# A decoder block's residual turnings sixteen steps apart, later retention scores, and one write and four reads for both tiles of a turning

## Chip, cores, metric

The kernel runs on one core of one Trainium2 chip. The metric is the device time of that core in microseconds (us). Times of several runs are given as their median; the trace comes from one further, profiled execution.

## What is computed

A decoder block for 256 tokens (S), model width 2048 (D) and FFN width 5632, all in float32:

```python
h = h + 0.5 * swiglu(rms_norm(h, ffn1_norm), ffn1_w_gate, ffn1_w_up, ffn1_w_down)
n = rms_norm(h, mix_norm)
rq, rk, rv, rg, sq, sk, sv = split(n @ w_in)
ret = silu(rg) * groupnorm(retention(rope(rq), rope(rk), rv)) * ret_gn_gain   # 8 heads
swa = sliding_window_attention(rope(sq), rope(sk), sv, swa_sinks)             # 16 heads, window 128
h = h + concat(ret, swa) @ w_out
h = h + memory_cross_attention(rms_norm(h, xa_norm), rms_norm(mem, mem_norm), xa_wq, xa_wkv, xa_wo)
h = h + 0.5 * swiglu(rms_norm(h, ffn2_norm), ffn2_w_gate, ffn2_w_up, ffn2_w_down)
out = rms_norm(h, final_norm)
# swiglu(x, g, u, d) = (silu(x @ g) * (x @ u)) @ d
```

## The kernel before

**A stream of weight steps.** All the large products are one list of 772 steps. A step takes one 128 x 1024 piece of a weight matrix (512 KB) and does 12 matmuls of 128x512: two halves of the tokens (t = 0, 1), two pieces of 128 rows, and three matmuls for each fp32 product. `three` (L470 to L472) multiplies the high part of the activations with the high part of the weights (`wh`), the high part with the rest of the weights (`wl`), and the rest of the activations (`lo` in a `blk` tile) with `wh`. A `Unit` is the 4 to 12 steps that fill one PSUM tile `acc` (two of them alternate); when it ends, its `done` function is called.

**Preparing weights.** SP issues the loads: one DMA of 1 MB for two steps, `load_pair` (L203) or `load` (L197), into one of three `wf` tiles. `split` makes `wh` by a ScalarE copy (L71) and `wl` by a VectorE subtraction (L76), three steps ahead of the step that uses them (LOOKAHEAD), with four buffers each. Steps follow each other in program order on TensorE, ScalarE, VectorE and SP: the engines' orders are set when the program is built and no instruction overtakes another on its engine.

**Everything else** is put between the steps by `later(delay, fn)`: `fn` is called, and its instructions get their place, `delay` steps after the step at which `later` was called. SP issues the DMAs of such tasks in that same order, between its weight loads.

**Crossings.** Projections come out with tokens on the partitions, and the next product wants features there. `cross` (L434) turns a pair of 128x512 tiles: VectorE transposes each in squares of 32x32 into a 2 KB tile of the pool `t2k` (L444), a step later SP writes the two tiles to DRAM boxes (L449, 256 KB each), two steps after the start SP issues four reads for each box (L456, 64 KB each), which put the squares in place, and five steps after the start (TURN) the function `then` uses the result. It is used by `to_h` (residual additions), `up_done` (each block of gate-up products of an FFN), `rqk_done` (retention queries and keys), `put_done` (cross-attention queries and keys) and `turn_h`: 54 crossings in all. `turn_h` turns the residual `h` back to tokens on partitions for the last norm; `begin_ffn2` puts its four calls at 6, 10, 14 and 18 steps after the last product of the cross-attention (`xa_wo`), so at the start of the second FFN.

**Other pieces that the text names.** `Norm.finish` computes a row scale per token and `Norm.spread` (L412) lays it out over the partitions: two VectorE products (L417) and two TensorE transposes (L418). In retention `rqk_done` rotates queries and keys with VectorE (L730, L733); two and three steps later `ret_scores` (L740) does the score matmuls (L742, L743) and masks them on VectorE (L746, L747); `rv_done`'s `half` does the value matmuls (L761 to L764). `swa_group` (L606) does the sliding-window attention with VectorE and ScalarE; the product that divides the weights by their sum is L639, and five steps later TensorE transposes the weights (L646). In the tail `very_last` writes eight output tiles (L1000), all from `t2k`.

**Pools.** `t2k` has 10 tiles of 2 KB per partition, `blk` 13 of 8 KB, `wf` 3 of 8 KB, `wh` and `wl` 4 of 4 KB each; in PSUM there are two `acc` and four `tmp`.

Of the kernel before, what the change touches and what calls it, by code (L numbers as in the profile page):

```python
# [39 lines left out]
def decoder_block(ctx: ExitStack, tc: tile.TileContext, a: dict, out: bass.AP):  # L40
# [20 lines left out]
    def t2k(dt=F32):  # L61
        return work.tile([P, 512], dt, tag="t2k", name=nm("t2k"), bufs=10)

# [26 lines left out]
    nc.vector.tensor_copy(identr, ident)  # L90
    ones = const.tile([P, P], F32, tag="ones", name="ones")
    nc.vector.memset(ones, 1.0)
# [265 lines left out]
    class Norm:  # L358
# [39 lines left out]
        def finish(self):  # L398

            x = self.sums  # L400
            nc.vector.tensor_tensor(x[:, :S], x[:, :S], x[:, S:], ALU.add)
            tp = tmp_ps()
            for t in range(2):
                nc.tensor.matmul(tp[:, t : t + 1], x[:, t * P : (t + 1) * P], ones[:, :1], start=True, stop=True)
            ms = sm(2, "ms")
            nc.vector.tensor_scalar(ms, tp[:, :2], 1.0 / D, EPS, ALU.mult, ALU.add)
            nc.gpsimd.tensor_tensor(self.rs, ms, mhalf[:, :2], ALU.pow)
            self.ready = True
            if self.spreads:
                later(3, self.spread)  # L410

        def spread(self):  # L412

            tp = tmp_ps()
            for t in range(2):
                rep = t2k()[:, :P]
                nc.vector.tensor_scalar(rep, ones, self.rs[:, t : t + 1], None, ALU.mult)  # L417
                nc.tensor.transpose(tp[:, t * P : (t + 1) * P], rep, ident)  # L418
            self.rows = work.tile([P, S], F32, tag="rows", name=nm("rows"), bufs=1)
            copy(self.rows, tp[:, :S])  # L420

# [11 lines left out]

    def cross(src, then, room=None, delay=TURN):  # L434

        room = [None, None] if room is None else room
        boxes = []  # L440
        out = []
        sq = [t2k() for _ in src]
        for x, v in zip(sq, src):
            nc.vector.transpose(x.rearrange("p (g q j) -> p q g j", g=4, q=4), squares_of(v))  # L444

        def write():
            for x in sq:
                boxes.append(dram.tile([P, 512], F32, tag="box", name=nm("box")))
                nc.sync.dma_start(boxes[-1], x)  # L449

        def read():
            for box, dst in zip(boxes, room):
                dst = t2k() if dst is None else dst
                far = box.rearrange("(i r) (g n) -> g r i n", i=4, g=4)
                for g in range(4):
                    nc.sync.dma_start(dst[32 * g : 32 * g + 32, :].rearrange("p (i n) -> p i n", i=4), far[g])  # L456
                out.append(dst.rearrange("p (i q j) -> p q i j", i=4, q=4))
        later(1, write)
        later(2, read)
        later(delay, lambda: then(out))  # L460

# [13 lines left out]
    def to_h(w, lhs, factor, blocks, norm=None, then=None):  # L475

        def done(acc, b):
# [11 lines left out]
            else:  # L489
                s = [t2k() for _ in range(2)]  # L490
                for t in range(2):
                    copy(s[t], acc[:, t, :], scale=factor)
                cross(s, add, s)
        for b in range(4):
            Unit(w, b, 512, lhs, lambda acc, b=b: done(acc, b), blocks, pair=True)

    def ffn(norm, w_gate, w_up, down):
# [12 lines left out]
        def up_done(b):  # L510
            def done(acc):
# [4 lines left out]
                def made(out):  # L516
                    acts[b] = halves_of(out, blk())
                cross(s, made, s)
            return done
# [193 lines left out]
    def rqk_done(g, which):  # L713
        def done(acc):
            def finish(out):
# [18 lines left out]
                if which == 1:  # L734
                    for i in range(4):
                        later(2 + i // 2, lambda i=i: ret_scores(g, i, qk))
            cross([acc[:, t, :] for t in range(2)], finish)
# [107 lines left out]
    def put_done(norm, dst, i, then=None):  # L845

        def done(acc):
            s = [scaled(acc, t, 512, norm) for t in range(2)]

            def made(out):  # L850
                dst[i] = halves_of(out, blk())
                if then is not None:
                    later(1, then)
            cross(s, made, s)
        return done
# [146 lines left out]
    def begin_ffn2(b):  # L1002
        if b == 3:
            for b in range(4):
                later(6 + 4 * b, lambda b=b: turn_h(b))

# [85 lines left out]
```

## Time and profile before

| | |
|---|---|
| three runs | 2198.17, 2200.80, 2201.48 us; median 2200.8 us |
| profiled execution | 2198.31 us; its span 2196.5 us |
| TensorE (PE) busy | 2175.0 us, 99% of the span |
| VectorE (DVE) busy | 1291.7 us, 59% |
| ScalarE (ACT) busy | 1027.5 us, 47% |
| TensorE's mean granted clock | 0.998 of full |
| moved by DMA | 472.04 MB, 215 GB/s in the mean |

The span runs from the first to the last record of the trace; the execution's own time includes what lies around it, here 1.8 us. An engine's busy time doesn't count the time in which it waits, or issues DMAs. SP has no busy time of this kind: its line in the views is its queue (SPq), with the time that the issuing instructions took, their waits not included.

### The profile page before, as it was taken

How to read it: one execution, taken by the hardware profiler on the slowest of the kernel's cores; microseconds unless marked ns; L12 is line 12 of the kernel's file. 1: busy time of each engine (PE TensorE's matmuls, PEld its weight loads, DVE VectorE, ACT ScalarE, POOL GpSimd, SP SyncE). 2: the span in 40 equal slices, each digit the busy share in tenths (PEclk: the TensorE clock that was granted, in tenths of full speed). 3: DMA queues.
4: the chain of work that ended last, by engine and by line, in shares of the span. 5: the costliest groups of instructions: out<-in, count | busy, mean ns of one | idle time of the engine just before them, and what ended most of it. 6: DMA issues, size and time to landing. Idle time of an engine off the chain costs nothing.

```text
span 2196.5 us, 25627 instructions
## 1 busy us (share of the span) xinstructions
PE 2175.0 (99%) x9844; PEld 1804.2 (82%) x9844; DVE 1291.7 (59%) x1536; ACT 1027.5 (47%) x1258; POOL 10.4 (0%) x17
## 2 busy tenths in 40 slices
PE   9999999999999999999999999999899999999998
PEld 7888888888888888888888888887788888888886
DVE  6555555455556778886775555575555544555554
ACT  6444444444445554544564544454444433444443
POOL 0000000000000000000000000000000000000000
PEclk9999999999999999999999999999999999999999
DMA  7766677667667555556867654676766655666663
GB/s 269 233 217 211 216 228 232 215 214 234 206 222 262 201 185 191 174 191 207 270 232 245 215 174 171 210 250 214 246 214 215 226 196 195 215 207 220 216 215 144
DMA packets 187451, 472.04 MB, mean 215 GB/s; under 512 B 15552, under 2 KB 71616, under 8 KB 187200
## 3 DMA queue, kind: packets, MB, share of 16 engines
q1 hardware_dynamic: 187040, 470.22, 63.7%
q8 instruction: 77, 1.26, 0.2%
q14 instruction: 46, 0.38, 0.1%
q10 hardware_dynamic: 288, 0.18, 0.0%
HBM read 439.93 MB, written 30.41 MB: 214 GB/s over the span
## 4 chain that ended last, share of the span: by engine, by line
PE 95%; DVE 2%; DMA 1%; issue 1%; ACT 0%; SPq 0%; ACTq 0%; POOLq 0%; POOL 0%; DVEq 0%
PE acc L471 31%; PE acc L472 31%; PE acc L470 31%; DMA wf<-in_ffn_w_up 1%; DVE wl L76 1%; PE tmp L471 0%; PE tmp L472 0%; PE tmp L470 0%; ACT wh L71 0%; PE tmp L646 0%; DMA t2k<-box 0%; PE tmp L620 0%; DVE t2k L730 0%; DVE t2k L444 0%; PE tmp L742 0%
## 5 line engine op out<-in xcount | busy, mean ns | idle before, releaser
L76 DVE TENSOR_TENSOR wl<-wf,wh 128x1024 fp32r<-128x1024 f32 (+1 forms) x776 | 942.8, 1217 | 810.0 <-ACT wh L71 803.0
L71 ACT ACTIVATE wh<-wf 128x1024 fp32r<-128x1024 f32 (+1 forms) x776 | 817.4, 1056 | 1014.1 <-PE acc L472 955.9
L470 PE MATMUL acc<-wh,blk 128*128 128x512 f32 (+1 forms) x3104 | 1208.1, 389 | 4.4 <-ACT wh L71 3.2
L471 PE MATMUL acc<-wl,blk 128*128 128x512 f32 (+1 forms) x3104 | 1206.4, 389 | 4.7 <-DVE wl L76 4.6
L472 PE MATMUL acc<-wh,blk 128*128 128x512 f32 (+1 forms) x3104 | 1205.9, 388 | 0.0
L471 PEld LDWEIGHTS acc<-wl,blk 128*128 128x128 f32 x3104 | 583.3, 188 | 125.4 <-DVE wl L76 6.8
L470 PEld LDWEIGHTS acc<-wh,blk 128*128 128x128 f32 x3104 | 583.3, 188 | 124.4 <-ACT wh L71 3.6
L472 PEld LDWEIGHTS acc<-wh,blk 128*128 128x128 f32 x3104 | 583.1, 188 | 120.7 <-DVE blk L356 0.4
L444 DVE STREAM_TRANSPOSE t2k<-t2k 128x512 f32<-128x512 f32 x76 | 49.4, 687 | 16.8 <-ACT t2k L71 16.8
L71 ACT ACTIVATE blk<-t2k 128x512 fp32r<-128x512 f32 (+2 forms) x74 | 44.8, 608 | 9.2 <-DMA t2k<-box 7.3
L76 DVE TENSOR_TENSOR blk<-t2k,blk 128x512 fp32r<-128x512 f32 (+1 forms) x66 | 44.2, 672 | 0.0
L507 ACT ACTIVATE t2k<-acc,n 128x512 f32<-128x512 f32 x44 | 27.9, 686 | 31.6 <-PE acc L472 31.5
L514 DVE SCALAR_TENSOR_TENSOR t2k<-acc,n,t2k 128x512 f32<-128x512 f32 x44 | 31.0, 746 | 15.6 <-PE acc L472 15.6
L71 ACT ACTIVATE blk<-tmp 128x512 fp32r<-128x512 f32 (+2 forms) x53 | 23.9, 459 | 27.5 <-DVE blk L76 19.0
L71 ACT ACTIVATE blk<-h,gains 128x256 fp32r<-128x256 f32 x64 | 27.3, 496 | 5.7 <-DVE h L481 5.7
L356 DVE SCALAR_TENSOR_TENSOR blk<-h,gains,blk 128x256 fp32r<-128x256 f32 x64 | 26.9, 479 | 1.7 <-ACT blk L71 1.7
L393 DVE TENSOR_TENSOR t2k<-t2k,t2k 128x512 f32<-128x512 f32 x35 | 24.0, 685 | 2.3 <-ACT t2k L389 1.0
L76 DVE TENSOR_TENSOR blk<-tmp,blk 64x256 fp32r<-64x256 f32 (+2 forms) x45 | 22.2, 494 | 4.8 <-ACT blk L71 4.5
L471 PE MATMUL tmp<-blk,blk 128*128 128x256 f32 (+1 forms) x80 | 22.6, 282 | 0.6 <-DVE blk L76 0.6
L472 PE MATMUL tmp<-blk,blk 128*128 128x256 f32 (+1 forms) x80 | 22.5, 282 | 0.0
L470 PE MATMUL tmp<-blk,blk 128*128 128x256 f32 (+1 forms) x80 | 22.5, 281 | 0.0
L481 DVE TENSOR_TENSOR h<-h,t2k 128x512 f32<-128x512 f32 x32 | 21.0, 684 | 0.0
(122 smaller groups left out, 433.0 us busy)
## 6 DMA issues: line engine op xcount, KB each, us to landing
wf<-in_ffn_w_down SPq DMA_DIRECT2D x88, 1024.0 KB, 4.9
wf<-in_ffn_w_gate SPq DMA_DIRECT2D x87, 1024.0 KB, 5.1
wf<-in_ffn_w_up SPq DMA_DIRECT2D x87, 1024.0 KB, 5.2
box<-t2k SPq DMA_DIRECT2D x108, 256.0 KB, 2.1
t2k<-box SPq DMA_DIRECT2D x432, 64.0 KB, 4.7
wf<-in_w_in_rqk SPq DMA_DIRECT2D x16, 1024.0 KB, 5.1
wf<-in_w_in_rvg SPq DMA_DIRECT2D x16, 1024.0 KB, 5.0
wf<-in_w_out SPq DMA_DIRECT2D x16, 1024.0 KB, 5.1
```

The lines of the kernel that those rows point to most:

```text
L71: return nc.scalar.activation(dst, src, AF.Copy, **kw)
L76: nc.vector.tensor_tensor(lo, src, hi, ALU.subtract)
L356: nc.vector.scalar_tensor_tensor(x[:, k, 1, :], v[:, k, :], g, x[:, k, 0, :], ALU.mult, ALU.subtract)
L393: nc.vector.tensor_tensor(self.sums, self.sums, y, ALU.add)
L444: nc.vector.transpose(x.rearrange("p (g q j) -> p q g j", g=4, q=4), squares_of(v))
L470: nc.tensor.matmul(o, ah, bh, start=start, stop=False)
L471: nc.tensor.matmul(o, ah, bl, start=False, stop=False)
L472: nc.tensor.matmul(o, al, bh, start=False, stop=stop)
L481: nc.vector.tensor_tensor(v, v, out[t], ALU.add)
L507: nc.scalar.activation(gated[b][t], acc[:, t, :], AF.Silu, scale=norm.scale(t))
L514: nc.vector.scalar_tensor_tensor(s[t], acc[:, t, :], norm.scale(t), s[t], ALU.mult, ALU.mult)
```

## The change

- `t2k` has 7 tiles instead of 10. A new pool, `t4k`, has two tiles of 128 x 2 x 512 (4 KB per partition).
- `cross` takes one `t4k` tile: both VectorE transposes go into it, one DMA writes it to one box of 512 KB, four DMAs of 128 KB read the box back into the same tile, and `then` works on it. The callers' own tiles are no longer passed as a place for the result.
- `spread` puts its two VectorE products into one tile at once and its transposes two steps later; `ones` has one column instead of 128 and is broadcast.
- `ret_scores` comes at 4 and 5 steps after the rotation instead of 2 and 3.
- `turn_h` comes at 19, 35, 51 and 67 steps after the last product of `xa_wo` instead of 6, 10, 14 and 18.

```diff
     def t2k(dt=F32):
-        return work.tile([P, 512], dt, tag="t2k", name=nm("t2k"), bufs=10)
+        return work.tile([P, 512], dt, tag="t2k", name=nm("t2k"), bufs=7)
...
-    ones = const.tile([P, P], F32, tag="ones", name="ones")
+    ones = const.tile([P, 1], F32, tag="ones", name="ones")
...
         def spread(self):
 
-            tp = tmp_ps()
+            rep = t2k()[:, :S]
             for t in range(2):
-                rep = t2k()[:, :P]
-                nc.vector.tensor_scalar(rep, ones, self.rs[:, t : t + 1], None, ALU.mult)
-                nc.tensor.transpose(tp[:, t * P : (t + 1) * P], rep, ident)
-            self.rows = work.tile([P, S], F32, tag="rows", name=nm("rows"), bufs=1)
-            copy(self.rows, tp[:, :S])
+                nc.vector.tensor_scalar(rep[:, t * P : (t + 1) * P], ones.broadcast_to([P, P]), self.rs[:, t : t + 1], None, ALU.mult)
+
+            def turned():
+                tp = tmp_ps()
+                for t in range(2):
+                    ts = slice(t * P, (t + 1) * P)
+                    nc.tensor.transpose(tp[:, ts], rep[:, ts], ident)
+                self.rows = work.tile([P, S], F32, tag="rows", name=nm("rows"), bufs=1)
+                copy(self.rows, tp[:, :S])
+            later(2, turned)
...
-    def cross(src, then, room=None, delay=TURN):
...
-        room = [None, None] if room is None else room
-        boxes = []
-        out = []
-        sq = [t2k() for _ in src]
-        for x, v in zip(sq, src):
-            nc.vector.transpose(x.rearrange("p (g q j) -> p q g j", g=4, q=4), squares_of(v))
+    def cross(src, then, delay=TURN):
...
+        z = work.tile([P, 2, 512], F32, tag="t4k", name=nm("t4k"), bufs=2)
+        for t, v in enumerate(src):
+            nc.vector.transpose(z[:, t, :].rearrange("p (g q j) -> p q g j", g=4, q=4), squares_of(v))
+        box = dram.tile([2 * P, 512], F32, tag="box", name=nm("box"))
 
         def write():
-            for x in sq:
-                boxes.append(dram.tile([P, 512], F32, tag="box", name=nm("box")))
-                nc.sync.dma_start(boxes[-1], x)
+            nc.sync.dma_start(box.rearrange("(t p) n -> p t n", t=2), z)
 
         def read():
-            for box, dst in zip(boxes, room):
-                dst = t2k() if dst is None else dst
-                far = box.rearrange("(i r) (g n) -> g r i n", i=4, g=4)
-                for g in range(4):
-                    nc.sync.dma_start(dst[32 * g : 32 * g + 32, :].rearrange("p (i n) -> p i n", i=4), far[g])
-                out.append(dst.rearrange("p (i q j) -> p q i j", i=4, q=4))
+            far = box.rearrange("(i r) (g n) -> g r i n", r=32, g=4)
+            for g in range(4):
+                nc.sync.dma_start(z[32 * g : 32 * g + 32].rearrange("p t (i n) -> p (t i) n", i=4), far[g])
         later(1, write)
         later(2, read)
-        later(delay, lambda: then(out))
+        later(delay, lambda: then([z[:, t, :].rearrange("p (i q j) -> p q i j", i=4, q=4) for t in range(2)]))
...
-                        later(2 + i // 2, lambda i=i: ret_scores(g, i, qk))
+                        later(4 + i // 2, lambda i=i: ret_scores(g, i, qk))
...
-                later(6 + 4 * b, lambda b=b: turn_h(b))
+                later(19 + 16 * b, lambda b=b: turn_h(b))
```

Lines move by one or two: the write is L450, the reads are L455, `ret_scores`' matmuls L740 and L741, its masks L744 and L745, the dividing product L637, its transposes L644.

On SP, at the start of the second FFN, the order before is this. L203 is a weight load, L449 a write and L456 the reads; 11554 and 11555 are the tiles of turning 0, and 11644 and 11645 those of turning 1.

```order
L203 DMA wf_11522<-in_ffn_w_gate 128x2x1024
L203 DMA wf_11562<-in_ffn_w_gate 128x2x1024
L449 DMA box_11576<-t2k_11554 128x512
L449 DMA box_11578<-t2k_11555 128x512
L456 DMA t2k_11596<-box_11576 32x4x128 x4
L456 DMA t2k_11601<-box_11578 32x4x128 x4
L203 DMA wf_11610<-in_ffn_w_gate 128x2x1024
L203 DMA wf_11652<-in_ffn_w_gate 128x2x1024
L449 DMA box_11672<-t2k_11644 128x512
L449 DMA box_11674<-t2k_11645 128x512
L456 DMA t2k_11695<-box_11672 32x4x128 x4
L456 DMA t2k_11700<-box_11674 32x4x128 x4
```

With the change it is this; 11346 is the first gate-up crossing of the second FFN and 11503 is turning 0.

```order
L450 DMA box_11349<-t4k_11346 128x2x512
L203 DMA wf_11372<-in_ffn_w_up 128x2x1024
L455 DMA t4k_11346<-box_11349 32x8x128 x4
L203 DMA wf_11410<-in_ffn_w_up 128x2x1024
L203 DMA wf_11449<-in_ffn_w_up 128x2x1024
L203 DMA wf_11483<-in_ffn_w_up 128x2x1024
L450 DMA box_11506<-t4k_11503 128x2x512
L203 DMA wf_11529<-in_ffn_w_gate 128x2x1024
L455 DMA t4k_11503<-box_11506 32x8x128 x4
```

A turning's reads stood directly behind its write, and two turnings stood two loads apart; now a load stands between write and reads, and four loads between the reads of one crossing and those of the next.

On VectorE, in the second group of retention heads, the order before is this. `t2k_7399` holds the sliding-window weights that L639 divides; L746 and L747 are masks of the scores, and the `wl` rows are weight splits.

```order
L747 TENSOR_TENSOR t2k_7465<-tmp_7462,blk_4727 128x128
L76 TENSOR_TENSOR wl_7469<-wf_7338,wh_7468 128x1024
L637 TENSOR_TENSOR den_7410<-den_7410,es_7411 128x2
L746 TENSOR_TENSOR t2k_7493<-tmp_7490,blk_4727 128x256
L638 RECIPROCAL den_7410<-den_7410 128x2
L747 TENSOR_TENSOR t2k_7493<-tmp_7490,blk_4727 128x128
L639 TENSOR_TENSOR t2k_7399<-t2k_7399,den_7410 128x512
L746 TENSOR_TENSOR t2k_7499<-tmp_7496,blk_4727 128x256
L747 TENSOR_TENSOR t2k_7499<-tmp_7496,blk_4727 128x128
L76 TENSOR_TENSOR wl_7503<-wf_7338,wh_7502 128x1024
```

With the change it is this; `t2k_7229` are the same weights, and L637 is the same product.

```order
L744 TENSOR_TENSOR t2k_7334<-tmp_7331,blk_4615 128x256
L745 TENSOR_TENSOR t2k_7334<-tmp_7331,blk_4615 128x128
L76 TENSOR_TENSOR wl_7338<-wf_7256,wh_7337 128x1024
L635 TENSOR_TENSOR den_7240<-den_7240,es_7241 128x2
L636 RECIPROCAL den_7240<-den_7240 128x2
L637 TENSOR_TENSOR t2k_7229<-t2k_7229,den_7240 128x512
L744 TENSOR_TENSOR t2k_7358<-tmp_7355,blk_4615 128x256
L745 TENSOR_TENSOR t2k_7358<-tmp_7355,blk_4615 128x128
L76 TENSOR_TENSOR wl_7377<-wf_7256,wh_7376 128x1024
```

The dividing product stands behind the 346th weight split of VectorE where it stood behind the 344th; the transposes L644 that read it stand at the same step of TensorE as L646 did.

## Rows read from the trace of the kernel before

**Rows 1.** Busy time by stretch: stretch; us, PE, PEld, DVE, ACT, POOL, clock, DMA, GB/s.
```profile
1130.00:1174.00 44.00, 44.00 (x196) 36.44 (x195) 28.07 (x34) 25.04 (x34) 0.00 (x0) 1.00 0.74 246
1486.00:1530.00 44.00, 44.00 (x195) 36.43 (x195) 23.88 (x26) 21.10 (x24) 0.52 (x1) 1.00 0.73 226
1530.00:1574.00 44.00, 36.44 (x150) 28.74 (x150) 21.39 (x22) 18.41 (x22) 0.00 (x0) 0.96 0.73 250
```

**Rows 2.** TensorE's timeline, 1520 to 1560: start, busy us, instruction, [wait before <-for].
```profile
1535.65 0.39 PE L472 MATMUL acc<-wh,blk 128*128 128x512 f32 x1
1539.19 0.50 PE L470 MATMUL acc<-wh,blk 128*128 128x512 f32 x1 [3.15 <-ACT wh L71]
...
1543.30 0.63 PE L470 MATMUL acc<-wh,blk 128*128 128x512 f32 x1
...
1556.83 0.50 PE L471 MATMUL acc<-wl,blk 128*128 128x512 f32 x1 [3.58 <-DVE wl L76]
```

**Rows 3.** SP's timeline, 1495 to 1560.
```profile
1501.75 1.25 SPq L449 DMA_DIRECT2D box<-t2k  x2
1510.92 3.64 SPq L456 DMA_DIRECT2D t2k<-box  x8
1514.66 0.85 SPq L449 DMA_DIRECT2D box<-t2k  x2
1515.60 0.40 SPq L203 DMA_DIRECT2D wf<-in_ffn_w_up  x1
```

**Rows 4.** Waits of SP's queue, 1486 to 1560: line <- waited for: us, times, longest.
```profile
SPq L456 <- DMA box<-t2k: 26.2, 5, 7.8
```

**Rows 5.** SP's timeline, 1130 to 1160.
```profile
1130.51 0.94 SPq L449 DMA_DIRECT2D box<-t2k  x2
1134.13 0.38 SPq L203 DMA_DIRECT2D wf<-in_xa_wk  x1
1134.61 5.29 SPq L456 DMA_DIRECT2D t2k<-box  x8
1140.05 8.03 SPq L203 DMA_DIRECT2D wf<-in_xa_wk  x3
```

**Rows 6.** TensorE's timeline, 760 to 762.
```profile
761.09 0.33 PE L418 MATMUL tmp<-ident,t2k 128*128 128x128 f32 x1 [0.53 <-DVE t2k L417]
```

**Rows 7.** TensorE's timeline, 860 to 863.
```profile
862.02 0.67 PE L742 MATMUL tmp<-blk 128*128 128x256 f32 x2 [0.68 <-DVE blk L733]
```

**Rows 8.** TensorE's timeline, 964 to 967.
```profile
965.70 0.67 PE L742 MATMUL tmp<-blk 128*128 128x256 f32 x2 [0.71 <-DVE blk L76]
```

**Rows 9.** DMA issues of the crossings: count, KB each, median us to landing.
```profile
box<-t2k SPq DMA_DIRECT2D x108, 256.0 KB, 2.1
t2k<-box SPq DMA_DIRECT2D x432, 64.0 KB, 4.7
```

**Rows 10.** Waits of ScalarE in the whole span.
```profile
ACT wh L71 <- PE acc L472: 955.9, 618, 3.6
...
ACT blk L71 <- DMA t2k<-box: 7.3, 7, 2.1
```

**Rows 11.** VectorE's timeline, 962 to 975.
```profile
971.18 0.68 DVE L639 TENSOR_TENSOR t2k<-t2k,den 128x512 f32<-128x512 f32 x1
...
972.32 1.22 DVE L76 TENSOR_TENSOR wl<-wf,wh 128x1024 fp32r<-128x1024 f32 x1
973.93 1.23 DVE L76 TENSOR_TENSOR wl<-wf,wh 128x1024 fp32r<-128x1024 f32 x1 [0.39 <-ACT wh L71]
```

**Rows 12.** TensorE's timeline, 966 to 980.
```profile
975.31 0.60 PE L646 MATMUL tmp<-ident,t2k 128*128 128x128 f32 x4
```

**Rows 13.** SP's timeline, 2180 to 2196.
```profile
2185.59 7.24 SPq L1000 DMA_DIRECT2D out<-t2k  x8
```

**Rows 14.** DMA issues of the output.
```profile
out<-t2k SPq DMA_DIRECT2D x8, 256.0 KB, 2.7
```

**Rows 15.** ScalarE's timeline, 2186 to 2196.
```profile
2190.52 1.33 ACT L71 ACTIVATE t2k<-blk,frs 128x512 f32<-128x512 f32 x2 [1.05 <-POOL frs L990]
```

More of the change, by code (lines that the diff above doesn't have):

```diff
@@ L403, in finish @@
             for t in range(2):
-                nc.tensor.matmul(tp[:, t : t + 1], x[:, t * P : (t + 1) * P], ones[:, :1], start=True, stop=True)
+                nc.tensor.matmul(tp[:, t : t + 1], x[:, t * P : (t + 1) * P], ones, start=True, stop=True)
             ms = sm(2, "ms")
@@ L492, in done @@
                     copy(s[t], acc[:, t, :], scale=factor)
-                cross(s, add, s)
+                cross(s, add)
         for b in range(4):
@@ L517, in made @@
                     acts[b] = halves_of(out, blk())
-                cross(s, made, s)
+                cross(s, made)
             return done
@@ L853, in made @@
                     later(1, then)
-            cross(s, made, s)
+            cross(s, made)
         return done
```

## The prediction

> **What bounds the kernel now.** I read four views in this order: busy time by stretch, the waits of TensorE, the timelines of TensorE and SP around the longest waits, and the waits of SP's queue. The first says that TensorE is the bound nearly everywhere. In an undisturbed stretch of 44 us (1130 to 1174) it is busy for all 44.00 us and starts 196 matmuls, one per 0.2245 us; a step of 12 is 2.7 us [rows 1]. Faster DMA, ScalarE or VectorE buy nothing there. A gain can only come from where TensorE waits, and the waits are few. From 1530 to 1574 the same 44 us hold 150 matmuls and 36.44 us of busy time, at a granted clock of 0.96; just before, from 1486 to 1530, still 195 [rows 1]. That one hole is worth (196 - 150) x 0.2245 = 10.3 us: 44.00 - 36.44 = 7.6 us idle, the other 2.8 us mostly matmuls at the lower clock. [...]
>
> [...] In the hole's run-up SP writes two boxes at 1501.75 and issues the reads only at 1510.92, and no weight load in between; after them it writes again at 1514.66 and only then, at 1515.60, loads [rows 3]. In 1486 to 1560 SP waits 26.2 us in 5 pieces for box writes to land, the longest 7.8 us [rows 4]. These are the four residual turnings, which now start four steps apart, and the gate-up turnings among them. The order of SP shows why the wait is long: a turning's write stands directly behind two 1 MB loads, and its reads directly behind the write, so SP stands until loads and write have landed, with all later loads queued behind it. A turning that stands well is in the undisturbed stretch: write at 1130.51, one load at 1134.13, reads at 1134.61, next loads from 1140.05, with TensorE never idle [rows 1, 5].
>
> Three smaller waits of TensorE are touched too: 0.53 us of the first transpose in `spread` for its VectorE input [rows 6], and 0.68 and 0.71 us of the first retention scores of each group, which VectorE's rotation holds up [rows 7, 8].
>
> **The change, part by part.**
>
> Residual turnings at 19 + 16b steps instead of 6 + 4b: they fall 8 steps from each gate-up turning. The changed order gives each of them write, load, reads, as in the undisturbed stretch, which also has a crossing every 8 steps. Nothing is added: the same four turnings with the same VectorE transposes and ScalarE copies. I take the whole hole: **-10.3 us**. From below: nothing gained, if SP is held as long in each new place; the five waits of 26.2 us [rows 4] could recur, but one at a time. From above it is 10.3, as the stretch then has no other loss. I take that end, for the undisturbed stretch is the nearest row.
>
> One write of 512 KB and four reads of 128 KB per crossing instead of two and eight: 54 crossings, so 54 x 5 = 270 DMAs fewer than the 108 and 432 there are [rows 9]. SP spends 5.29 us on eight reads of a crossing [rows 5]; four at 5.29 / 8 = 0.66 us or less are 2.6 us, so SP is free some 2.6 us earlier. Outside the hole this is hidden: TensorE is busy all the time around such crossings [rows 1], so **0**. If the cover were gone, 2.6 us a crossing is the most it could return. Against it, the first tile can be used only when both have landed. The waits of ScalarE for read tiles are 7.3 us in 7 places so far [rows 10]; a microsecond more at each of the 54 would be hidden as well, because ScalarE waits 955.9 us in 618 places for TensorE to free a split buffer, so it runs as far ahead as its four buffers let it, up to three steps or 8 us. 0 again; cost if that lead is gone: 1 us a crossing.
>
> Scores two steps later (5.4 us): both waits of 0.68 and 0.71 us end: **-1.4 us** (at most; the nearest rows are the waits themselves, and more cannot be gained there). What is late next is the masked score products that the second half's value matmuls need. In the changed order the last of these VectorE products stand before the value matmuls by a step and more, so I count nothing.
>
> `spread` split in two: the same two VectorE products, now into one tile, and the transposes two steps later: 0.53 us goes, **-0.5 us**; between nothing and 0.5. `ones` of one column instead of 128 saves a part of one VectorE memset, 0. The changed broadcast read of it is no row before; two products of 128 columns can hardly cost or save more than 0.5 us together, and not on TensorE's path.
>
> A new wait. In the second group the product that normalises the attention weights (L639, now L637) stands two weight splits further down in VectorE's order than before, while TensorE's transposes of it stay at the same step. Before, it ends at 971.18 + 0.68 = 971.9 and the transposes start at 975.31 [rows 11, 12]: 3.4 us to spare. Behind the next two splits, which end at 973.93 + 1.23 = 975.2, it would end at 975.9. That is 0.6 us too late, and up to 1.4 if TensorE comes 0.7 us earlier. Bounds 0 and 1.5 us; I take **+0.8 us**, between the two readings.
>
> Smaller pool (7 tiles of 2 KB instead of 10): crossings no longer hold tiles of it, which is what makes room. In the changed order only one reuse in the retention stretch has no distance, a score tile behind transposes that TensorE runs in the same step, some 0.5 us on VectorE, which the lead above covers. At the end, the second half's outputs take over tiles whose output DMAs were issued from 2185.59 on; the third starts two places later at 7.24 / 8 = 0.9 us each, so at 2187.4, and lands some 2.7 us after that, at 2190.1, and ScalarE writes from 2190.52 [rows 13 to 15]: 0, with less than 0.5 us to spare. [...]
>
> Sum: -10.3 - 1.4 - 0.5 + 0.8 = **-11.4 us**. The profiled execution took 2198.3 us (span 2196.5), so 2186.9 us. It is near the fastest of the three runs (2198.17); the median, 2200.8, lies 2.5 us higher, which no view explains. From the median the sum gives 2189.4; I take the middle, **2188 us**.
>
> **The rivals.**
>
> 1. Half of the hole stays. For it: loads still queue in front of a write when SP has fallen behind, and each turning still blocks SP while its write lands. Against: single turnings 16 steps apart have 43 us to recover, and the undisturbed stretch shows no loss. -11.4 + 5.2 = -6.2 us: 2192 to 2195 us.
> 2. The order is changed but the time isn't: the DMA traffic of the turnings costs the same spread over four places (2.6 us each), or the spacing only uncovers another late load. For it: in the hole the DMA engines were no busier than in the undisturbed stretch, so bytes could be needed as much there. Against: [rows 1] once more. Only 1.1 us remain: 2197 to 2200 us.
> 3. Slower: the seven-tile pool becomes the bound in the retention stretch, 750 to 1010 us, where score tiles, values and attention tiles live together. Each of some 32 hand-overs from VectorE to TensorE there (12 transposes, 8 scores, 8 values, 4 products) could wait as the two score rows do, 0.7 us: 22 us, which gives 2198.3 - 11.4 + 22 = 2209 us. It decides from the point where over 23 of them wait (11.4 + 4.4 = 15.8 us). Against: one close reuse in the order, not dozens. [...]
>
> **How the numbers follow.** Forecast 0.76, half a hole 0.11, no change 0.08, slower 0.05. A difference under 0.2% (4.4 us) is about what a measurement of this kernel can't tell from none. The first two are faster, so faster 0.87, same 0.08, slower 0.05. The forecast's own range is 2184 (the fast runs' level, no new wait, and up to 1 us more from DMA) to 2190; with half a hole it reaches to 2194. What is left out is rivals 2 and 3 and the tails.
>
> **What would show it.** Right: 1530 to 1574 as full as 1130 to 1174, granted clock 1.00 there; SP's waits for box writes near 0 in the second FFN's start; five DMAs per crossing; no TensorE wait at the scores or `spread`; a wait of about a microsecond at the attention transposes near 973. Wrong: late splits after a residual turning, TensorE waits for VectorE repeated all over 750 to 1010, or ScalarE and VectorE standing for read tiles long enough that splits come late.

## The result and the profile after

The changed kernel takes 2186.14 us (median of four runs, 2185.94 to 2187.13), the kernel before 2200.99 us in the same comparison (2198.17 to 2201.48). The ratio is 0.9936, with an interval from 0.9919 to 0.9953: 14.9 us less, where 2188 us were forecast, inside the range of 2184 to 2194 us. The profiled execution took 2187.13 us with a span of 2185.3 us, so trace against trace the gain is 2196.5 - 2185.3 = 11.2 us, where the sum of the prediction had 11.4.

TensorE's waits, over the whole span of the changed kernel (engine, tile and line, what it waited for: us in all, times, longest):

```profile
PE acc L468 <- ACT blk L71: 2.2, 2, 2.0
PE tmp L95 <- POOL ident masks.py:199: 1.4, 1, 1.4
PE tmp L469 <- DVE blk L76: 0.6, 1, 0.6
```

Nothing is left of the waits for `wh` and `wl` of [rows 2], nor of those at `spread` and the scores of [rows 6 to 8]. The first two rows stand at the start, the second before any load has landed; the third, at 842 us, stood there before the change too.

Busy time by stretch, with the columns of [rows 1]:

```profile
1486.00:1530.00 44.00, 44.00 (x195) 36.41 (x194) 24.26 (x24) 21.95 (x24) 0.47 (x1) 1.00 0.70 231
1530.00:1574.00 44.00, 44.00 (x195) 36.41 (x194) 24.53 (x24) 20.70 (x23) 0.00 (x0) 1.00 0.75 243
```

SP's timeline at turning 0, in the place of [rows 3]:

```profile
1524.95 0.37 SPq L450 DMA_DIRECT2D box<-t4k  x1
1527.61 0.37 SPq L203 DMA_DIRECT2D wf<-in_ffn_w_gate  x1
1528.72 1.81 SPq L455 DMA_DIRECT2D t4k<-box  x4
1531.89 11.25 SPq L203 DMA_DIRECT2D wf<-in_ffn_w_gate  x3
```

The waits of SP's queue from 1486 to 1662, in the place of [rows 4]:

```profile
SPq L455 <- DMA box<-t4k: 7.8, 6, 1.7
```

The stretch that held 150 matmuls now holds 195, at full clock, with the DMA traffic of the undisturbed stretch (a share of 0.75 and 243 GB/s, against 0.74 and 246 [rows 1]). A turning now reads as the undisturbed crossing of [rows 5] does: write, load, reads, three loads. SP waits for box writes 7.8 us in all from 1486 to 1662, the longest 1.7 us; the kernel before waits 26.2 us in the 74 us of [rows 4] alone, the longest 7.8 us. The crossings' DMAs, in the place of [rows 9]:

```profile
box<-t4k SPq DMA_DIRECT2D x54, 512.0 KB, 3.1
t4k<-box SPq DMA_DIRECT2D x216, 128.0 KB, 5.1
```

They are 270 fewer, and each takes a little longer to land than those of half the size (2.1 and 4.7 us).

Where the 11.2 us lie is found by comparing the same place of the same weight step, the start of its second matmul, in both traces:

| steps | before | after | difference |
|---|---|---|---|
| the span's start to step 20 | 64.15 | 65.58 | +1.43 |
| 20 to 260 | 652.80 | 652.80 | 0 |
| 260 to 290, `spread` | 88.73 | 87.88 | -0.85 |
| 290 to 325, first scores | 114.93 | 114.01 | -0.92 |
| 325 to 350, second scores | 81.27 | 80.44 | -0.83 |
| 350 to 455, cross-attention | 304.12 | 304.62 | +0.50 |
| 455 to 525 | 199.80 | 199.77 | -0.03 |
| 525 to 550, the hole | 78.37 | 68.00 | -10.37 |
| 550 to 771 | 601.25 | 601.25 | 0 |

They sum to -11.07 us; the rest, 0.1 us, lies behind step 771. Below, the **hole** of a kernel is the time of the steps 525 to 550 less the 68.0 us (25 x 2.72) that they take here.

### The profile page after: what moved, and what is told of

The parts are those of the page before. It is cut to its first block, busy times and chain, and to the rows that moved or that the text cites. A ratio compares the mean times of both kernels' runs of the same rounds, so it can differ in the third digit from the quotient of the medians.

```text
span 2185.3 us, 25094 instructions
## 1 busy us (share of the span) xinstructions
PE 2172.8 (99%) x9844; PEld 1805.2 (83%) x9844; DVE 1291.7 (59%) x1536; ACT 1027.4 (47%) x1258; POOL 9.5 (0%) x17
## 4 chain that ended last, share of the span: by engine, by line
PE 98%; DVE 0%; DMA 0%; issue 0%; ACT 0%; SPq 0%; ACTq 0%; POOLq 0%; POOL 0%
PE acc L468 32%; PE acc L469 32%; PE acc L470 32%; PE tmp L470 0%; PE tmp L469 0%; PE tmp L468 0%; DMA wf<-in_ffn_w_gate 0%; PE tmp L644 0%; PE tmp L618 0%; PE tmp L740 0%; PE tmp L694 0%; PE tmp L404 0%; PE tmp L762 0%; PE tmp L761 0%; PE tmp L759 0%
## 5 line engine op out<-in xcount | busy, mean ns | idle before, releaser
L446 DVE STREAM_TRANSPOSE t4k<-t2k 128x512 f32<-128x512 f32 x76 | 49.3, 687 | 15.3 <-ACT t2k L71 15.3
L71 ACT ACTIVATE blk<-t4k 128x512 fp32r<-128x512 f32 (+1 forms) x68 | 38.6, 614 | 0.9 <-DMA t4k<-box 0.9
L76 DVE TENSOR_TENSOR blk<-t4k,blk 128x512 fp32r<-128x512 f32 x60 | 38.6, 684 | 0.3 <-ACT blk L71 0.3
L389 ACT ACTIVATE t2k<-h 128x512 f32<-128x512 f32 x32 | 18.2, 617 | 6.2 <-DVE h L479 6.2
```

The lines of the kernel that those rows point to most:

```text
L71: return nc.scalar.activation(dst, src, AF.Copy, **kw)
L76: nc.vector.tensor_tensor(lo, src, hi, ALU.subtract)
L389: nc.scalar.activation(y.rearrange("p (k s) -> p k s", k=2), v[:, k : k + 2, :], AF.Square)
L446: nc.vector.transpose(z[:, t, :].rearrange("p (g q j) -> p q g j", g=4, q=4), squares_of(v))
```

## Experiments

Each is compared with the kernel before on the same chip. Differences of under some 4 us between medians tell nothing by themselves; there the hole and the waits of the trace are read.

### 1. The kernel before, again

> The kernel before once more, for a second trace of the hole. Its medians lie 2.7 us above its profiled execution (2200.99 against 2198.31 us), and no view told why. If the size of the hole varies from run to run (10.4 us in the first trace), this trace shows another size, up to some 13 us, and the rest of the stream alike. If the hole is fixed and the start or the tail varies, the hole is within 0.3 us of 10.4 us and the difference stands before 25 us or after 2170 us. Time 2198 to 2202 us either way.

No edit. Median 2201.31 us (2198.21 to 2203.24), ratio 0.9998, interval 0.9990 to 1.0007. The profiled execution took 2203.24 us; its start is 1.8 us longer than in the first trace, its hole 13.7 us instead of 10.4. TensorE's rows there (start, duration, in brackets the wait):

```profile
1540.56 0.58 PE L470 MATMUL acc<-wh,blk 128*128 128x512 f32 x1 [3.01 <-ACT wh L71]
1541.82 0.79 PE L471 MATMUL acc<-wl,blk 128*128 128x512 f32 x1 [0.68 <-DVE wl L76]
1542.41 0.63 PE L472 MATMUL acc<-wh,blk 128*128 128x512 f32 x1
...
1547.11 0.63 PE L471 MATMUL acc<-wl,blk 128*128 128x512 f32 x1
...
1559.34 0.79 PE L471 MATMUL acc<-wl,blk 128*128 128x512 f32 x1 [3.60 <-DVE wl L76]
...
1564.20 0.63 PE L470 MATMUL acc<-wh,blk 128*128 128x512 f32 x1
```

Two more rows of the first trace, beside those of [rows 2]; the second stands directly behind the wait of 3.58 us:

```profile
1540.45 0.50 PE L471 MATMUL acc<-wl,blk 128*128 128x512 f32 x1 [0.76 <-DVE wl L76]
...
1557.17 0.40 PE L472 MATMUL acc<-wh,blk 128*128 128x512 f32 x1
```

Busy time in the stretch of the hole, with the columns of [rows 1]:

```profile
1530.00:1574.00 44.00, 36.72 (x136) 28.65 (x135) 19.20 (x20) 17.59 (x20) 0.00 (x0) 0.84 0.70 231
```

The waits are those of the first trace, 3.01, 0.68 and 3.60 us for 3.15, 0.76 and 3.58. What differs is the clock behind them: here 12 matmuls in a row take 0.63 us from 1542.41 to 1547.11 and 11 more behind the second long wait; in the first trace 7 did behind the first, at a granted clock of 0.50 from 1541.6 to 1544.5, and none behind the second. The mean granted clock behind the second wait, from 1556 to 1566, was 1.00 of full in the first trace and 0.66 here. So the hole costs 10 to 14 us for nearly the same waits, and more where the mean granted clock from 1530 to 1574 is lower: 10.4 us at 0.96 and 13.7 us at 0.84 in these two traces, and 13.2 us at 0.88 and 11.7 us at 0.92 in the two later ones that have it whole, of experiments 8 and 12. The first trace of before was one of the cheap ones, near the fastest of its runs. That is the part of the 2.5 us between profile and median that no view of one trace could show; the start, which varies by 2 to 3 us between traces, is the other.

### 2. Only the turnings sixteen steps apart

```diff
-                later(6 + 4 * b, lambda b=b: turn_h(b))
+                later(19 + 16 * b, lambda b=b: turn_h(b))
```

> The kernel before with the turnings at 19 + 16b steps and nothing else. My theory: the hole ends with this part alone, so 10.4 us less than the kernel before in the trace, 2188 us in a profiled execution, 195 or 196 matmuls in each 44 us from 1486 to 1662, and the waits at spread and at both score groups stay (0.5, 0.7, 0.7 us). Rival (the crossing in one write and four reads is what frees SP): half of the hole or more stays, 2193 us or later. Rival (the turnings' cost is only spread out): four losses of 2 us or more behind the turnings, 2196 us or later.

2188.77 us (2187.72 to 2189.95) against 2201.21 us; ratio 0.9946, interval 0.9932 to 0.9960. Hole 0.0 us; the profiled execution took 2187.72 us, 10.6 us less than the first trace. The waits at `spread` and the scores are all there (0.5, 0.7, 0.7 us). This one line is the gain of the change but for 2 to 3 us.

### 3. Sixteen apart, but reads directly behind the write

```diff
-                later(6 + 4 * b, lambda b=b: turn_h(b))
+                later(18 + 16 * b, lambda b=b: turn_h(b))
```

> The kernel before with the turnings at 18 + 16b: as far apart as in the run before, but each read directly behind its write on SP, with no load between. If the order of write and read on SP decides, each of the four turnings costs some of what it did: 4 x 2.6 us, so 2196 to 2199 us. If the distance decides, SP still waits some 6 us at each of the four writes (24 us in all) but the lead of the weights takes it up, TensorE loses nothing, and the time is that of the run before, 2188 us.

2188.83 us, ratio 0.9944, interval 0.9932 to 0.9956: the time of experiment 2. SP's timeline at a turning:

```profile
1523.50 0.37 SPq L203 DMA_DIRECT2D wf<-in_ffn_w_up  x1
1524.12 0.94 SPq L449 DMA_DIRECT2D box<-t2k  x2
1530.21 3.64 SPq L456 DMA_DIRECT2D t2k<-box  x8
1533.94 6.24 SPq L203 DMA_DIRECT2D wf<-in_ffn_w_gate  x3
```

The waits of its queue from 1486 to 1662:

```profile
SPq L456 <- DMA box<-t2k: 21.2, 5, 5.2
```

The write stands behind a load, the reads wait for it 5 us with nothing issued between, and TensorE loses nothing: the hole is 0.0 us. One such stand is taken up by the weights that lie ready; the order on SP alone costs nothing. The stands are not all as long as in the kernel before: there SP, once late, issues two loads directly ahead of the write of the second and of the fourth turning, and stands over 7 us at their reads.

### 4. Four apart, but with a load between write and reads

```diff
-                later(6 + 4 * b, lambda b=b: turn_h(b))
+                later(7 + 4 * b, lambda b=b: turn_h(b))
```

> The kernel before with the turnings at 7 + 4b: as close as before, but with a load between write and read for three of them (turning 1 falls together with a gate-up crossing: four writes, a load, sixteen reads). If the order on SP decides, most of the hole ends: under 3 us lost, 2188 to 2191 us. If the distance decides, six crossings in twenty steps hold SP and the DMA queues as long, and 6 us or more of the hole stay: 2194 to 2199 us.

2188.26 us, ratio 0.9943, interval 0.9931 to 0.9956. The hole is 0.3 us. SP's timeline at a turning:

```profile
1523.44 1.09 SPq L449 DMA_DIRECT2D box<-t2k  x2
1524.63 0.39 SPq L203 DMA_DIRECT2D wf<-in_ffn_w_up  x1
1525.82 7.38 SPq L456 DMA_DIRECT2D t2k<-box  x8
1533.30 0.40 SPq L203 DMA_DIRECT2D wf<-in_ffn_w_up  x1
```

Busy time in the stretch of the hole:

```profile
1530.00:1574.00 44.00, 44.00 (x195) 36.04 (x194) 24.90 (x25) 22.72 (x28) 0.00 (x0) 1.00 0.83 272
```

The waits of SP's queue from 1486 to 1662:

```profile
SPq L456 <- DMA box<-t2k: 3.9, 3, 2.6
```

The 3.9 us are not all that SP waits at the reads: the same view names a weight load as what ended another 9.8 us of them (experiment 6 shows such a wait). The turnings are as close as before and 272 GB/s move, more than in any stretch of the kernel before shown here; TensorE stays busy. So it is not the bytes either. But it is close: in steps 536 to 542 the split of `wl` ends between 0.06 and 0.34 us ahead of its use in every second step, where it has 4.5 to 5.9 us in an undisturbed stretch. Two conditions made the hole, turnings four steps apart **and** reads directly behind a write that stands behind loads; either alone costs 0.3 us or less, and the change takes away both.

### 5. Everything but the crossing's new form

The kernel before with the new `spread` and these lines:

```diff
-                        later(2 + i // 2, lambda i=i: ret_scores(g, i, qk))
+                        later(4 + i // 2, lambda i=i: ret_scores(g, i, qk))
...
-                later(6 + 4 * b, lambda b=b: turn_h(b))
+                later(19 + 16 * b, lambda b=b: turn_h(b))
```

> The kernel before with the turnings at 19 + 16b, the scores at 4 and 5 steps and the new spread, but with its old crossings (two writes, eight reads, ten tiles of 2 KB). My theory: one write and four reads are worth nothing where SP isn't behind, so this is the changed kernel within 1 us: 2185.5 to 2187.5 us, with the waits of TensorE at spread and at both score groups gone (2.6 us below the turnings alone, 2188.8 us). Rival (SP's 2.6 us a crossing do reach TensorE somewhere): over 1.5 us slower than the changed kernel.

2186.37 us (2184.82 to 2186.50) against 2199.60 us, ratio 0.9938, interval 0.9926 to 0.9951; the changed kernel has 2186.14 us. One write and four reads instead of two and eight, and ten tiles instead of seven and two, make no difference that can be measured. In the trace the old crossing is even better by a little: the steps 420 to 455 of the cross-attention take 111.68 us here and 111.65 in experiment 2, but 112.06, 112.05 and 112.05 us in the changed kernel and experiments 6 and 7, the three with the new crossing.

### 6. Only the crossing's new form

The changed kernel with the turnings at 6 + 4b, the scores at 2 and 3 steps and the old `spread` (`ones` stays one column wide).

> The kernel before with the new crossings (one write, four reads, two tiles of 4 KB, seven of 2 KB; ones of one column, which makes the room) and nothing else: turnings at 6 + 4b, scores at 2 and 3 steps, the old spread. My theory: the reads still stand directly behind the writes and the turnings four steps apart, so most of the hole stays, 7 us or more, and the time is 2196 to 2202 us; the two tiles may add a wait, as four turnings and the gate-up crossings between them want three at once. Rival (SP's time per crossing made the hole): SP spends half as long on reads, and 5 us or more of the hole go: 2196 us or less.

2195.33 us (2194.08 to 2197.17) against 2199.60 us, ratio 0.9981, interval 0.9972 to 0.9990. The hole is 6.7 us, a little under the 7 that I had expected to stay, and the time lies in the rival's range. The waits of SP's queue from 1486 to 1662:

```profile
SPq L450 <- DMA box<-t4k: 39.5, 8, 9.4
```

Busy time in the stretch of the hole:

```profile
1530.00:1574.00 44.00, 39.96 (x166) 31.81 (x166) 22.56 (x23) 18.80 (x21) 0.00 (x0) 0.96 0.77 265
```

SP waits longer for writes than before (39.5 us against 30.2 in this stretch of the kernel before), so the mechanism stands; and yet 3.7 us of the hole of the first trace are gone, and with them the first long wait of TensorE (3.15 us in [rows 2]). The likely reason is how long a crossing's reads hold SP, which counts where SP is late. At the gate-up crossing within the hole, in the kernel before and here:

```profile
1516.80 4.78 SPq L456 DMA_DIRECT2D t2k<-box  x8
1515.98 1.80 SPq L450 DMA_DIRECT2D t4k<-box  x4
```

The next load follows at 1521.98 us there and at 1517.88 here. So the reads hold SP 5.2 us there and 1.9 here. Some 1.8 us of the difference are issue time, as eight reads take 3.64 us where nothing holds them [rows 3]. The rest is mostly a wait of the eighth read for the weight load ahead of the reads, 1.3 us at this crossing of the kernel before (waits of SP's queue, 1516 to 1522). In the kernel before, at 46 of the 47 crossings whose reads follow a load directly, the eighth read is issued 0.02 us after the load has landed, 1.7 us after the seventh in the median. That the shorter hold, and not the landing of fewer DMAs, returned the 3.7 us wasn't tried apart.

### 7. One tile of 4 KB instead of two

```diff
-        z = work.tile([P, 2, 512], F32, tag="t4k", name=nm("t4k"), bufs=2)
+        z = work.tile([P, 2, 512], F32, tag="t4k", name=nm("t4k"), bufs=1)
```

> The changed kernel with one tile of 4 KB instead of two. Crossings stand 8 steps apart nearly everywhere and hold the tile for some 5, so one tile is enough there: within 1 us of the changed kernel (2186.1 us) but for the places where two stand closer than 5 steps (the end of the cross-attention's output product, the start of an FFN), where VectorE's transpose waits and up to 3 us could be lost each. If tiles bound the crossings everywhere, 54 crossings lose a microsecond or more each: 2240 us.

2187.65 us, ratio 0.9947, interval 0.9934 to 0.9961. One wait of TensorE is new, 1.2 us for a `wl` split at the end of the cross-attention's output product; the steps 455 to 525 take 201.26 us instead of 199.77. The rest is as in the changed kernel. Tiles of 4 KB don't bind the crossings.

### 8. The kernel before with seven tiles of 2 KB

```diff
-        return work.tile([P, 512], dt, tag="t2k", name=nm("t2k"), bufs=10)
+        return work.tile([P, 512], dt, tag="t2k", name=nm("t2k"), bufs=7)
```

> The kernel before with seven tiles of 2 KB instead of ten, its crossings still in them: the third rival's shortage made on purpose, for a crossing then holds two to four of the seven. If a shortage of tiles shows as the same short wait of TensorE repeated in the retention stretch, 750 to 1010 us, some 32 hand-overs of 0.7 us would cost 22 us there: 2220 us. If ScalarE's and VectorE's lead takes it up, the stretch costs under 2 us more and the time is 2199 to 2205 us, and then the seven tiles of the changed kernel, whose crossings don't use them, are further from costing anything.

2200.95 us against 2199.60 us, ratio 1.0006, interval 0.9997 to 1.0015. TensorE's waits from 750 to 1010 us:

```profile
PE tmp L742 <- DVE blk L733: 0.7, 1, 0.7
PE tmp L471 <- DVE blk L76: 0.6, 1, 0.6
PE tmp L742 <- DVE blk L76: 0.5, 1, 0.5
PE tmp L418 <- DVE t2k L417: 0.2, 1, 0.2
```

They are the waits of the kernel before, none more; the hole is 13.2 us, within what it varies by. The third rival has no ground, though here the crossings take their tiles from the seven as well. Three tiles less cost nothing; that seven tiles would be short was the rival's own assumption.

### 9. The turnings on GpSimd's queue

```diff
-    def cross(src, then, room=None, delay=TURN):
+    def cross(src, then, room=None, delay=TURN, queue=nc.sync):
...
-                nc.sync.dma_start(boxes[-1], x)
+                queue.dma_start(boxes[-1], x)
```

The reads take `queue` likewise, and `turn_h` passes `nc.gpsimd`.

> The kernel before with its turnings where they were, four steps apart, but their writes and reads issued by GpSimd's queue instead of SP's, so that no weight load stands behind a read that waits for its write. The same bytes move at the same time. If SP's standing still makes the hole, it goes: under 1 us lost between 1486 and 1574 and 2187 to 2190 us, and GpSimd waits for the writes in SP's place. If the bytes of six crossings in twenty steps made the weights late, whoever issues them, 6 us or more stay: 2194 us or later.

2194.84 us against 2202.69 us, ratio 0.9964, interval 0.9952 to 0.9977. The hole is 6.4 us: half of it stays, which I had not expected. The waits of SP's queue from 1486 to 1662:

```profile
SPq L456 <- DMA box<-t2k: 0.9, 1, 0.9
```

GpSimd's waits in the same stretch:

```profile
POOL t2k L456 <- DMA box<-t2k: 10.2, 2, 6.2
```

ScalarE's timeline at the third turning:

```profile
1533.10 0.63 ACT L71 ACTIVATE blk<-t2k 128x512 f32<-128x512 f32 x1 [6.31 <-DMA box<-t2k]
```

SP no longer stands for the turnings: 0.9 us. Now GpSimd stands for the writes. The view names ScalarE for its waits at the reads of the first and the fourth turning, 5.2 and 5.5 us, but in the trace those reads too are issued 0.6 to 0.7 us after the first of the two writes has landed. The reads land late, and ScalarE, whose program has the copy of the turned tile ahead of the next weight splits, stands 6.31 us at it; the copy starts when the fourth read of its tile has landed, at 1533.03 us, and not with a write, as its row says.

### 10. The sliding-window values a step later

```diff
-                later(4, lambda: swa_values(g, t, heads[-1] // 4, probs))
+                later(5, lambda: swa_values(g, t, heads[-1] // 4, probs))
```

> The changed kernel with the sliding-window value products one step later (5 instead of 4). TensorE's last wait within the stream, 0.6 us at 842 us for a split by VectorE, should end: 0.6 us off the trace, 2185.5 us. That is less than the 0.2% a measurement tells from no change; the waits of TensorE decide. If something else is late at that place, the same wait stands a step later and nothing is gained.

2185.45 us (2185.07 to 2186.98), against 2186.14 us of the changed kernel in another comparison. TensorE's waits within the stream:

```profile
PE tmp L469 <- DVE blk L76: 0.7, 1, 0.7
```

The wait is still there. The first value matmul moved by a step, but the VectorE split that the second one waits for stands where it stood, behind eight products of the rotation (L727 to L731, until 842.3 us in the changed kernel). Nothing is gained; the 0.7 us between the medians is within their spread, and the steps 0 to 20 are 1.9 us shorter in this trace.

### 11. GpSimd's queue, and the turned tiles used later

Experiment 9 with one more edit in `turn_h`:

```diff
-        cross([hT[b][:, :, t * P : (t + 1) * P].rearrange("p q (a j) -> p q a j", a=4) for t in range(2)], made, queue=nc.gpsimd)
+        cross([hT[b][:, :, t * P : (t + 1) * P].rearrange("p q (a j) -> p q a j", a=4) for t in range(2)], made, delay=8, queue=nc.gpsimd)
```

> The turnings where they were, issued by GpSimd's queue as in the run before, and ScalarE's copies of the turned tiles eight steps after the start instead of five. In the run before, SP no longer stood for the writes and half of the hole stayed; ScalarE stood 6.3 us at a copy whose reads were late, with the weight splits behind it. If that stand is what was left, it goes: under 1.5 us lost, 2187 to 2190 us. If the bytes of the crossings make the weights late, the hole stays at 5 us or more: 2194 us.

2188.01 us (2187.85 to 2192.17) against 2200.70 us, ratio 0.9945, interval 0.9932 to 0.9959. By the median the hole is gone; in the profiled execution (2189.98 us) 3.4 us of it are left, half of experiment 9 and more than the 1.5 us expected. ScalarE's waits from 1486 to 1574:

```profile
ACT blk L71 <- DMA t2k<-box: 19.1, 6, 6.1
```

Busy time in the stretch of the hole:

```profile
1530.00:1574.00 44.00, 41.48 (x181) 33.48 (x180) 21.52 (x21) 19.61 (x23) 5.48 (x10) 1.00 0.77 243
```

ScalarE still stands for read tiles, 19.1 us in six places; eight steps are not enough for reads that go by GpSimd's queue. That its stand is all that was left isn't shown; that using the tiles later takes away half of it is.

### 12. SP's queue, and the turned tiles used later

```diff
-        cross([hT[b][:, :, t * P : (t + 1) * P].rearrange("p q (a j) -> p q a j", a=4) for t in range(2)], made)
+        cross([hT[b][:, :, t * P : (t + 1) * P].rearrange("p q (a j) -> p q a j", a=4) for t in range(2)], made, delay=8)
```

> The kernel before with ScalarE's copies of the turned tiles eight steps after the start instead of five; SP issues everything in the order and at the steps it did. If SP's standing for the writes makes the hole, as I hold, most of it stays, 7 us or more: 2197 us or later. If ScalarE's standing at those copies (6.6 us in five places in the first trace) made it, it goes: 2190 us or less.

2200.32 us (2196.96 to 2203.01) against 2200.70 us, ratio 0.9999, interval 0.9990 to 1.0008; the hole is 11.7 us. The waits of SP's queue from 1486 to 1662:

```profile
SPq L456 <- DMA box<-t2k: 29.4, 6, 7.1
```

ScalarE's waits from 1486 to 1574:

```profile
ACT wh L71 <- DMA wf<-in_ffn_w_up: 15.6, 3, 6.6
ACT wh L71 <- DMA wf<-in_ffn_w_gate: 9.9, 2, 7.7
```

Busy time in the stretch of the hole:

```profile
1530.00:1574.00 44.00, 36.67 (x144) 28.84 (x143) 20.55 (x21) 16.97 (x21) 0.00 (x0) 0.92 0.75 254
```

ScalarE no longer waits for a read tile anywhere in the stretch; it waits 25.5 us for weights. With ScalarE's stand taken away the whole hole stays; with SP's stands at the writes cut short and the turnings as close (experiment 4) it goes. So in the kernel before it is SP's stand that makes it. With the stand moved to GpSimd (experiment 9) ScalarE's takes its place at half the price.

## Why the prediction was right

**The hole, -10.3 us: right in cause, and in size against this trace; the cause was narrower than put.** The term measured -10.37 us, trace against trace, but that trace of before was a cheap one: the other three with the whole hole show 11.7 to 13.7. The cause was that SP stands for writes that stand behind 1 MB loads, with all later loads queued behind it: shown by experiments 2, 4 and 12 together. The prediction leaned on the new order of write, load and reads as much as on the distance; experiments 3 and 4 show that either would have done. In the trace of before, SP's reads waited up to 7.8 us for writes, and the loads behind them were issued only after the reads [rows 3, 4]. What reached TensorE were late splits: its two long waits, 3.15 and 3.58 us, are for `wh` and `wl` [rows 2], and ScalarE, which makes `wh`, waited for weight loads 11.3 us (`in_ffn_w_up`) and 6.2 us (`in_ffn_w_gate`) from 1486 to 1574.

**The crossing's new form, 0: right.** Experiment 5 shows it, 2186.37 against 2186.14 us. The prediction also named the price where the cover is gone, at most 2.6 us a crossing. That bound was too low: it took the 5.29 us of [rows 5] for issue time, but they hold the eighth read's wait for a load, 1.6 us of them. In the median of 54 crossings the reads hold SP 5.4 us in the kernel before and 1.8 us in the changed one, some 3.5 us less; experiment 6 shows a place without cover, where 3.7 us of the hole went. Outside the hole, halving the number of the transfers bought nothing because TensorE had no wait for it to shorten.

**The scores, -1.4 us: right in kind, low by 0.35.** The steps show -0.92 and -0.83 us. The waits of [rows 7, 8] are idle time of the engine's record only; the matmuls on both sides of a wait stood 0.16 us further apart than the usual 0.23 us and the wait in brackets add up to.

**`spread`, -0.5 us: low for the same reason,** -0.85 us measured.

**The new wait at the attention transposes, +0.8 us: this step failed.** VectorE's timeline in the changed kernel:

```profile
971.10 1.22 DVE L76 TENSOR_TENSOR wl<-wf,wh 128x1024 fp32r<-128x1024 f32 x1
972.24 0.15 DVE L635 TENSOR_TENSOR den<-den,es 128x2 f32<-128x2 f32 x1
972.42 0.17 DVE L636 RECIPROCAL den<-den 128x2 f32<-128x2 f32 x1
972.62 0.69 DVE L637 TENSOR_TENSOR t2k<-t2k,den 128x512 f32<-128x512 f32 x1
```

TensorE's:

```profile
973.46 0.63 PE L644 MATMUL tmp<-ident,t2k 128*128 128x128 f32 x4
```

The product ends at 972.62 + 0.69 = 973.31 us and the transposes start at 973.46: 0.15 us to spare, where it was 3.4 us [rows 11, 12]. The margin did go, as forecast, but nothing was lost. The step set the product behind the two splits at the times that they had in the kernel before, where the masks of all four scores stand ahead of both splits on VectorE. In the changed order only two scores' masks stand ahead of the second split, and none between the product and the splits, so that split ends at 972.32 instead of 975.2.

**Seven tiles, 0: right.** Experiment 8 shows it, with the crossings in the same pool.

**Not foreseen: the start.** This trace loses 1.43 us in the first 20 steps, and its row there is:

```profile
9.57 0.79 PE L468 MATMUL acc<-wh,blk 128*128 128x512 f32 x1 [1.97 <-ACT blk L71]
```

It is no effect of the change: the steps 0 to 20 take 63.85, 65.77, 63.97 and 65.91 us in experiments 2, 3, 4 and 1, which have the same start as the kernel before. It put this profiled execution at the slow end of its four runs, as the cheap hole had put that of before at the fast end. The four traces that have the hole whole show 10.4, 13.7, 13.2 and 11.7 us, 12.2 in the mean; with that in place of 10.37, and with no difference at the start, the rows of the table sum to -14.4 us. That is how a gain of 11.2 us between the traces and of 14.9 us between the medians go together, and why the middle between the two readings, 2188 us, came out 1.9 us too high: most of the median's surplus was a dearer hole, which the change removes.

**Not foreseen: the cross-attention, +0.5 us,** of which the new crossing has some 0.4 (experiment 5). The prediction had put the delay of the first tile until both have landed at nothing, as hidden, and so it was: TensorE has no wait there. What differs is TensorE's order, here in the changed kernel:

```profile
1209.59 0.39 PE L468 MATMUL acc<-wh,blk 128*128 128x512 f32 x1
1209.82 0.38 PE L470 MATMUL tmp<-blk,blk 128*128 128x256 f32 x1
```

The first matmul of the next weight step stands between the second and the third product of the attention's scores, and from that third product to the next it takes 0.22 us, where it takes 0.12 between the others. This is so at all four attentions of the changed kernel and of experiments 6, 7 and 10, and at none where the crossing is the old one: 4 x 0.1 us. Why the order came out so isn't shown.

**That the sum came so close to the traces is luck.** The terms missed 1.6 us of gain (0.07 at the hole, 0.35 each at the scores and `spread`, 0.8 for a wait that didn't come), and the start and the cross-attention, which it didn't foresee, cost 1.9 us. So -11.4 stood against -11.2 us.

## What to carry to other kernels

Look for what stands behind a waiting instruction in its queue, not for the wait itself: 21 us of waits on SP in 176 us cost nothing when they came one at a time (experiment 3), and 26 us in 74 us cost 10 to 14 us when the next came before the lead of the weights was made up. Spacing such work out, or putting an independent load between its two halves, each cured it; moving it to another queue moved the stand and kept half of the loss (6.4 us, experiment 9). And the hole had no fixed price, 10.4 to 13.7 us in four traces at mean granted clocks of 0.96 to 0.84, so one trace of it was one draw: compare medians with a second trace in hand.

## What the runs showed of the hardware

Waits of the same length were followed by a lower granted clock in one execution and not in another: behind 3.58 us of waiting the next matmuls took 0.39 to 0.40 us in the first trace of before (its row is in experiment 1), at a granted clock of 1.00 from 1556 to 1566, and behind 3.60 us, at the same instruction, 11 in a row took 0.63 us in the second, at a mean of 0.66 in the same window (experiment 1). The hole differed by 3.3 us, while the waits for splits in it differed by 0.2 us. In the kernel before, a box write of 256 KB landed 2.0 to 3.8 us after its issue at the 98 writes ahead of which SP had issued no load within 1.6 us, 6.2 to 6.5 us at the six with one 1 MB load there, and 8.4 to 9.3 us at the four with two. At 46 of the 47 crossings whose reads follow a load directly, the eighth read was issued 0.02 us after that load had landed, 1.7 us after the seventh in the median (kernel before, experiment 6).
